# Gate loads moved to GpSimd's queue with five slots, three slots of gate scratch, and eight filler steps ahead of each attention loop, in a two-layer hybrid block

## The chip, the cores and the metric

The kernel runs on one core of one Trainium2 chip. The metric is the device time of one execution in microseconds; the number that stands for a kernel is the median of several runs. Engines are written as in the profile: PE (TensorE's matmuls), PEld (its weight loads), DVE (VectorE), ACT (ScalarE), POOL (GpSimd) and SP (SyncE, which only issues DMAs here).

## What is computed

Two layers of a hybrid block over 768 tokens (256 of context, 512 of latent), 1024 wide, in float32. Each layer projects the modulated input once, runs four mixers on slices of it, gates each by SiLU, and merges the four by per-channel sigmoid gates. In the second layer only the latent tokens are needed.

```python
def hybrid_layer(...):
    p = modulate(x, shift, scale) @ in_w          # split into the inputs of all four mixers
    oa = softmax_attention(mla_project(...))      # i=0, "mla"
    ob = rwkv_branch(...)                         # i=1, a scan over time in both directions
    oc = softmax_attention(gqa_project(...))      # i=2, "gqa"
    od = differential_attention(...)              # i=3, "diff": two softmaxes per head
    outs = [o * silu(gate) for o in (oa, ob, oc, od)]
    x_new = post_norm(ALPHA * x + gate_l * merge_branches(outs, logits, merge_b, branch_w, out_w))

def merge_branches(outs, gate_logits, merge_b, branch_w, out_w):
    g = jax.nn.sigmoid(gate_logits + merge_b)
    y = g[..., :D_MODEL] * (outs[0] @ branch_w[0])
    for i in range(1, N_BRANCH):
        y = y + g[..., i * D_MODEL:(i + 1) * D_MODEL] * (outs[i] @ branch_w[i])
    return y @ out_w
```

## The kernel before, in words

Every float32 product is made of three matmuls on a rounded high part and a low rest of each operand (`mm3`, L302; the same by hand in `m_block`, L539, and `m_stream`, L572). Weights come by DMA in pieces of 128x1024 on SP's queue; ACT rounds them (L292) and DVE takes the rest (L295).

A layer has three stages.

**Attention.** Three loops run one after the other, gqa, mla and diff. Ahead of each, `m_stream` projects its queries, keys and values (L572). In a loop PE transposes queries and keys (L601), makes scores (L647), DVE takes the row maximum (L650), ACT the exponential (L653), in the diff loop DVE combines two softmaxes (L962 to L964), PE transposes the weights (L669), ACT copies them (L671) and PE multiplies by the values (L694). Beside this runs a *filler*, one generator `fill()` for the whole stage: the input projections of the RWKV mixer (`t_block`, L302 with 256 or 512 columns, evicted at L986), in the first layer also the modulation for later (`ada`, L392), then the SiLU gates of the gqa and of the mla branch (`out_gate`, L539, 24 matmuls of 256 columns for each pair of token tiles and half of the weights). The filler has one PSUM bank, "F". `beside(loop, filler, FILL[l][n])` takes filler steps in proportion to the loop's steps; a step is 12 matmuls of 256 or of 512 columns, or 4 of L392. An order on each engine is then made by the scheduler from the order in which the program is traced: earlier traced goes first when both could.

**Scan.** The RWKV recurrence runs by an order of PE that is written out (`manual_schedule`), with a stream of other projections between its steps: the gates of diff (`out_gate` i=3) and of the scan's branch (`late_gate`), each with a scratch tile `oth`, and the merge gates (`merge_gates`), whose 32 tiles of 128x768 (128x512 in the second layer) are written to DRAM as `gd`.

**Merges.** `merge(i)` for i = 0, 2, 3, beside `rwkv_finish`, then i = 1. For each of eight column blocks j it loads the gate tile `th` from `gd` (three slots), every second j a weight tile `wb` (L1471; ACT L1472, DVE L1473), runs 12 matmuls of 384 columns (6 of 512 in the second layer) and lets DVE multiply by the gate (L1481 or L1483) and DVE or POOL add to `y` (L1484). At the end of `rwkv_finish` the tiles `h` are loaded on POOL's queue (L1654, six of 512 KB, four in the second layer), as soon as the memory of the scan is free. Then the output projection follows.

The change touches `out_gate`, `late_gate`, `merge` and `_run_layers`.

Of the kernel before, what the change touches and what calls it, by code (L numbers as in the profile page):

```python
# [10 lines left out]
F32 = mybir.dt.float32  # L11
F32R = mybir.dt.float32r
# [21 lines left out]
WBUFS = 5  # L34
LEAD = (6, 1, 6)
RATE = (2.15, 1.08)
# [176 lines left out]
class _Kernel:  # L213
# [1205 lines left out]
    def out_gate(self, l, i, O, toks, pool):  # L1419

        def use(t, g):
            th = self.t(pool, [128, 772 if pool is self.ep else 256], "E" if pool is self.ep else "oth")[:, :256]
            self.gate(th, g)
            self.nc.gpsimd.tensor_tensor(out=O[:, t], in0=O[:, t], in1=th, op=ALU.mult)
        yield from self.m_block(l, f"og{i}", toks, use)

    def late_gate(self, l, i, toks):

        def use(t, g):
            th = self.t(self.mp, [128, 256], "oth")  # L1430
            self.gate(th, g)
            self.nc.scalar.dma_start(out=self.gg[t], in_=th)
        yield from self.m_block(l, f"og{i}", toks, use)
# [14 lines left out]
    def merge(self, l, i, O, toks, y, first):  # L1448

        nc = self.nc  # L1450
        base, n = toks[0] * 128, len(toks) * 128
# [13 lines left out]
        for j in range(8):  # L1465
            th = self.t(self.mp, [128, n], "th", bufs=3)
            nc.sync.dma_start(out=th, in_=self.gd[i * 8 + j][:, :n])
            if j % 2 == 0:
                o = (i * 8 + j) * 256
                raw, wh, wl = (self.t(self.mp, [128, 512], f"wb{x}", F32R if x else F32, bufs=2) for x in range(3))  # L1470
                nc.sync.dma_start(out=raw, in_=self.a["brw"][l][:, o:o + 512])  # L1471
# [62 lines left out]
def _run_layers(K, only=None):  # L1534
# [18 lines left out]
    for l in range(DEPTH):  # L1553
# [23 lines left out]
        with mk(f"qk{l}", QB) as K.qp, mk(f"ep{l}", EB) as K.ep, mk(f"at{l}") as K.ap, \  # L1577
# [4 lines left out]
            filler = K.with_bank(fill(), "F")  # L1582

            def free():
                while K.wbusy:
                    next(filler, None)
            Qg = K.gq_proj(l, qt)
            Kg, Vg, kr = K.gkv_proj(l)
            O[2] = newO()
            beside(K.gqa_attn(qt, O[2], Qg, Kg, Vg), filler, FILL[l][0])  # L1590
            free()
            ready.add(2)
            m = K.mla_proj(l, qt, kr)
            O[0] = newO()
            beside(K.mla_attn(qt, O[0], *m), filler, FILL[l][1])
            free()
            ready.add(0)
            dd = K.diff_proj(l, qt)
            O[3] = newO()
            beside(K.diff_attn(l, qt, O[3], *dd), filler, FILL[l][2])  # L1600
            run(filler)
# [128 lines left out]
```

## Time and profile before

| | |
|---|---|
| median of 3 runs | 2085.11 us (2085.06 to 2086.12) |
| the profiled execution | 2084.66 us |
| its span on the core | 2082.9 us |
| PE busy | 1903.6 us (91%) |
| DVE busy | 1156.1 us (56%) |
| ACT busy | 816.6 us (39%) |
| POOL busy | 181.2 us (9%) |
| mean granted clock of TensorE | 0.962 |

The stages, in us from the span's start: first layer attention 50 to 531 (gqa loop from 84, mla from 245, diff from 383), scan to 980, merges to 1107, output projection to 1176; second layer attention 1200 to 1585 (gqa loop from 1239, mla from 1339, diff from 1482), scan to 1940, merges to 2026, output projection to the end. PE is busy almost everywhere, so the question at each place is how much of a stretch PE does not work, what it waits for, and at which clock it works.

### The profile page before, as it was taken

To read this page: it belongs to the slowest core of one execution; us is meant where nothing else is said; L and a number is where in the kernel's file an instruction comes from. 1 tells how busy PE (TensorE), PEld (TensorE's weight loads), DVE (VectorE), ACT (ScalarE), POOL (GpSimd) and SP (SyncE) were. 2 spreads that over 40 slices of the span, in tenths; PEclk is the share of its full clock that TensorE was granted. 3 is DMA by queue.
4 is the path that set the end of the run, shared out by engine and by line. 5 is a ranking of instruction groups with operands and counts; after the bars stand their busy time and mean duration, and the time that the engine had idled before them with its cause. 6 is when DMAs were issued, how large, how long until landed. Compare 5 with 4: busy or idle time off the path is not lost. (4 is left out here: it accounts for less than half of the span.)

```text
span 2082.9 us, 46213 instructions
## 1 busy us (share of the span) xinstructions
PE 1903.6 (91%) x19886; PEld 1575.2 (76%) x19886; DVE 1156.1 (56%) x2471; ACT 816.6 (39%) x1649; POOL 181.2 (9%) x303
## 2 busy tenths in 40 slices
PE   6899999888899999999788979999988999999877
PEld 4778878666788898888676677788877777777556
DVE  5554453576434433443878865454686444445677
ACT  3454462565323332332122236463665343233230
POOL 1000000000200000000130020000101000000120
PEclk9899999998899999999999889999998999999989
DMA  7110133310222222223743220111102222222651
GB/s 281 37 31 28 57 93 91 91 53 21 65 85 73 72 73 73 73 73 122 249 143 116 100 65 21 44 41 31 42 21 82 81 88 83 77 89 78 230 165 41
DMA packets 62614, 176.04 MB, mean 85 GB/s; under 512 B 7449, under 2 KB 12233, under 8 KB 62409
## 3 DMA queue, kind: packets, MB, share of 16 engines
q1 hardware_dynamic: 47144, 139.93, 21.4%
q10 hardware_dynamic: 13824, 27.90, 3.8%
q0 software_dynamic: 1440, 5.24, 0.6%
q8 instruction: 156, 2.56, 0.5%
q14 instruction: 50, 0.40, 0.1%
HBM read 145.50 MB, written 27.55 MB: 83 GB/s over the span
## 5 line engine op out<-in xcount | busy, mean ns | idle before, releaser
L302 PE MATMUL ps<-xh,wx 128*128 128x384 f32 (+2 forms) x3096 | 691.4, 368 | 4.0 <-ACT mth L1443 1.7
L302 PEld LDWEIGHTS ps<-xh,wx 128*128 128x128 f32 x3096 | 531.7, 189 | 65.8 <-issue 8.3
L292 ACT ACTIVATE wx<-wx 128x1024 fp32r<-128x1024 f32 (+2 forms) x94 | 98.3, 1046 | 307.1 <-PE ps L302 205.7
L295 DVE TENSOR_TENSOR wx<-wx,wx 128x1024 fp32r<-128x1024 f32 (+2 forms) x94 | 113.5, 1208 | 143.9 <-ACT wx L292 143.3
L650 DVE TENSOR_REDUCE nmax<-ps 128x1 f32<-128x768 f32 (+1 forms) x160 | 134.7, 846 | 54.8 <-PE ps L647 53.8
L572 PE MATMUL ps<-wx,xh 128*128 128x256 f32 (+1 forms) x1200 | 155.7, 288 | 7.6 <-DVE mu L1001 6.7
L302 PE MATMUL ps<-xh,wb 128*128 128x384 f32 (+1 forms) x576 | 134.3, 385 | 28.4 <-DVE th L1483 21.2
L572 PEld LDWEIGHTS ps<-wx,xh 128*128 128x128 f32 x1200 | 151.2, 191 | 9.6 <-ACT xc L476 6.8
L539 PE MATMUL ps<-wx,xh 128*128 128x256 f32 x960 | 139.9, 299 | 14.5 <-DVE oth L1417 7.4
L647 PE MATMUL ps<-qk,qk 128*128 128x384 f32 (+1 forms) x504 | 134.8, 371 | 16.7 <-ACT E L653 16.4
L653 ACT ACTIVATE E<-ps,nmax 128x768 f32<-128x768 f32 (+1 forms) x160 | 130.5, 817 | 44.2 <-DVE nmax L650 41.6
L302 PEld LDWEIGHTS ps<-xh,wb 128*128 128x128 f32 x576 | 107.6, 201 | 51.5 <-DVE th L1483 16.0
L539 PEld LDWEIGHTS ps<-wx,xh 128*128 128x128 f32 x960 | 128.7, 201 | 20.3 <-DVE oth L1417 7.8
L671 ACT ACTIVATE PH<-ps 128x512 f32<-128x512 f32 x156 | 91.1, 597 | 71.8 <-PE ps L669 71.3
L647 PEld LDWEIGHTS ps<-qk,qk 128*128 128x128 f32 x504 | 83.7, 195 | 40.7 <-ACT E L653 28.6
L1443 ACT ACTIVATE mth<-ps,hmb 128x384 f32<-128x384 f32 (+1 forms) x96 | 58.6, 611 | 113.1 <-PE ps L302 111.5
L669 PE MATMUL ps<-cstalways,E 128*128 128x128 f32 x624 | 99.9, 282 | 3.0 <-ACT PH L671 1.6
L694 PE MATMUL ps<-PH,V 128*64 128x256 f32 x624 | 88.1, 411 | 3.8 <-ACT PH L671 3.4
L669 PEld LDWEIGHTS ps<-cstalways,E 128*128 128x128 f32 x624 | 74.6, 144 | 15.9 <-ACT PH L671 4.6
L629 DVE TENSOR_TENSOR qk<-ps,qk 32x256 fp32r<-32x256 f32 (+5 forms) x104 | 59.3, 575 | 44.8 <-ACT qk L628 43.1
L295 DVE TENSOR_TENSOR wx<-wf,wx 128x1024 fp32r<-128x1024 f32 (+2 forms) x34 | 40.0, 1178 | 60.4 <-PE ps L302 33.8
L694 PEld LDWEIGHTS ps<-PH,V 128*64 128x64 f32 x624 | 41.8, 143 | 36.5 <-ACT PH L671 14.1
(325 smaller groups left out, 2782.2 us busy)
## 6 DMA issues: line engine op xcount, KB each, us to landing
wx<-in_inw_dram SPq DMA_DIRECT2D x88, 512.0 KB, 3.8
wf<-in_inw_dram SPq DMA_DIRECT2D x30, 512.0 KB, 3.6
wf<-in_adaw_dram SPq DMA_DIRECT2D x24, 512.0 KB, 3.6
gd<-mth ACTq DMA_DIRECT2D x32, 384.0 KB, 2.4
th<-gd SPq DMA_DIRECT2D x32, 384.0 KB, 3.2
adaw<-in_adaw_dram SPq DMA_DIRECT2D x16, 512.0 KB, 10.2
wx<-in_outw_dram SPq DMA_DIRECT2D x16, 512.0 KB, 4.8
wb<-in_brw_dram SPq DMA_DIRECT2D x32, 256.0 KB, 3.5
```

Of the source, the lines that this page charges most:

```text
L292: nc.scalar.activation(out=hi[:, :n], in_=raw[:, :n], func=AF.Copy)
L295: eng.tensor_tensor(out=lo[:, :n], in0=raw[:, :n], in1=hi[:, :n].bitcast(F32), op=ALU.subtract)
L302: self.nc.tensor.matmul(o, lhsT=w, rhs=x[:, s] if s is not None else x, start=first and p == 0, stop=last and p == 2)
L539: self.nc.tensor.matmul(ps[:, j * n:j * n + n], lhsT=self.xtok(x[k], s), rhs=w, start=k == 0 and p == 0 and j == 0, stop=k == 7 and p == 2 ...
L572: self.nc.tensor.matmul(ps, lhsT=self.xtok(x[k], s), rhs=w[:, c], start=k == 0 and p == 0 and head, stop=k == 7 and p == 2 and (tail or t ...
L629: nc.vector.tensor_tensor(out=lo[r, s], in0=ps[r], in1=hi[r, s].bitcast(F32), op=ALU.subtract)
L647: nc.tensor.matmul(o, lhsT=qt[:n, q], rhs=kt[:n, s], start=i == 0, stop=i == len(passes) - 1)
L650: nc.vector.tensor_reduce(out=nm, in_=v, axis=AX.X if ctx else AX.XY, op=ALU.max, negate=True)
L653: nc.scalar.activation(out=self.halves(e[:, :n], v), in_=v, func=AF.Exp, bias=nm, accum_out=den)
L669: nc.tensor.transpose(pt[:, c:c + 128], e[:, (k0 + k) * 128:(k0 + k) * 128 + 128], self.ident)
L671: nc.scalar.activation(out=hi, in_=pt, func=AF.Copy)
L694: nc.tensor.matmul(po[64 * (kk % 2):64 * (kk % 2) + 64, :n], lhsT=v2(kk), rhs=x[:, s], start=j == 0 and k < 2, stop=j == len(groups) - 1 a ...
```

## The change

Three things, in seven lines of code.

1. `LEAD` gets a fourth entry, 8, and a helper `ahead()` draws that many filler steps before each of the three attention loops, in both layers.
2. The scratch tile `oth` of the gates in the scan stage gets three slots instead of one.
3. In `merge`, the loads of the gate tiles `th` are issued on GpSimd's queue instead of SP's and get five slots instead of three; the high and low parts of the weight tile `wb` get three slots instead of two.

```diff
-LEAD = (6, 1, 6)
+LEAD = (6, 1, 6, 8)
...
     def out_gate(self, l, i, O, toks, pool):
...
-            th = self.t(pool, [128, 772 if pool is self.ep else 256], "E" if pool is self.ep else "oth")[:, :256]
+            th = self.t(pool, [128, 772], "E")[:, :256] if pool is self.ep else self.t(pool, [128, 256], "oth", bufs=3)
...
     def late_gate(self, l, i, toks):
...
-            th = self.t(self.mp, [128, 256], "oth")
+            th = self.t(self.mp, [128, 256], "oth", bufs=3)
...
     def merge(self, l, i, O, toks, y, first):
...
-            th = self.t(self.mp, [128, n], "th", bufs=3)
-            nc.sync.dma_start(out=th, in_=self.gd[i * 8 + j][:, :n])
+            th = self.t(self.mp, [128, n], "th", bufs=5)
+            nc.gpsimd.dma_start(out=th, in_=self.gd[i * 8 + j][:, :n])
...
-                raw, wh, wl = (self.t(self.mp, [128, 512], f"wb{x}", F32R if x else F32, bufs=2) for x in range(3))
+                raw, wh, wl = (self.t(self.mp, [128, 512], f"wb{x}", F32R if x else F32, bufs=3 if x else 2) for x in range(3))
...
+            def ahead():
+                for _ in range(LEAD[3]):
+                    next(filler, None)
...
+            ahead()
             beside(K.gqa_attn(qt, O[2], Qg, Kg, Vg), filler, FILL[l][0])
...
+            ahead()
             beside(K.mla_attn(qt, O[0], *m), filler, FILL[l][1])
...
+            ahead()
             beside(K.diff_attn(l, qt, O[3], *dd), filler, FILL[l][2])
```

Three places show how the order of the instructions changes.

PE at the start of the first layer's gqa loop, before. `ps_968` and `ps_1059` are filler (a projection of 256 and the next of 512 columns), `ps_913` and `ps_918` are query tiles and `ps_957` a key tile being transposed.

```order
L302 MATMUL ps_968<-xh_452,wx_964 128x256
L601 MATMUL ps_913<-cstalways_113,E_909 128x128 x2
L601 MATMUL ps_918<-cstalways_113,E_909 128x128 x4
L302 MATMUL ps_1059<-xh_239,wx_963 128x512
L302 MATMUL ps_1059<-xh_240,wx_963 128x512
L601 MATMUL ps_957<-cstalways_113,E_954 128x128 x2
```

The same place now; `ps_970` is the filler of 512 columns, `ps_993` and `ps_998` the queries, `ps_1014` the first keys.

```order
L302 MATMUL ps_970<-xh_387,wx_939 128x512
L302 MATMUL ps_970<-xh_386,wx_940 128x512
L601 MATMUL ps_993<-cstalways_113,E_989 128x128 x2
L601 MATMUL ps_998<-cstalways_113,E_989 128x128 x4
L302 MATMUL ps_970<-xh_437,wx_939 128x512
L302 MATMUL ps_970<-xh_438,wx_939 128x512
L302 MATMUL ps_970<-xh_437,wx_940 128x512
L302 MATMUL ps_970<-xh_452,wx_939 128x512
L302 MATMUL ps_970<-xh_453,wx_939 128x512
L302 MATMUL ps_970<-xh_452,wx_940 128x512
L601 MATMUL ps_1014<-cstalways_113,E_1011 128x128 x2
```

Of the 24 matmuls of 512 columns, 2 stood ahead of the first keys; now all 24 do, 18 of them ahead of the queries too. In the second layer the numbers are 0 ahead of the first keys and now 18, with the other 6 behind the first keys.

PE inside the second layer's diff loop, before. L539 is filler (a SiLU gate), the rest is the loop.

```order
L539 MATMUL ps_16394<-wx_16384,xh_13172 128x256
L647 MATMUL ps_16341<-qk_16112,qk_16152 128x384 x2
L539 MATMUL ps_16394<-wx_16383,xh_13174 128x256
L694 MATMUL ps_16283<-PH_16270,V_2663_15559 64x256 x2
L694 MATMUL ps_16283<-PH_16250,V_2663_15559 64x256 x2
L694 MATMUL ps_16283<-PH_16232,V_2663_15559 64x256 x2
L647 MATMUL ps_16365<-qk_16170,qk_16212 128x384
L601 MATMUL ps_16294<-cstalways_113,E_16290 128x128 x2
L601 MATMUL ps_16306<-cstalways_113,E_16290 128x128 x4
L647 MATMUL ps_16365<-qk_16170,qk_16212 128x384
L539 MATMUL ps_16394<-wx_16383,xh_13198 128x256
L539 MATMUL ps_16394<-wx_16384,xh_13198 128x256
```

The same heads and tiles now.

```order
L647 MATMUL ps_16593<-qk_16400,qk_16434 128x384 x2
L694 MATMUL ps_16545<-PH_16532,V_2680_15746 64x256 x2
L694 MATMUL ps_16545<-PH_16518,V_2680_15746 64x256 x2
L694 MATMUL ps_16545<-PH_16500,V_2680_15746 64x256 x2
L647 MATMUL ps_16617<-qk_16452,qk_16486 128x384
L601 MATMUL ps_16556<-cstalways_113,E_16552 128x128 x2
L601 MATMUL ps_16562<-cstalways_113,E_16552 128x128 x4
L647 MATMUL ps_16617<-qk_16452,qk_16486 128x384
```

The filler is gone from the whole of this loop: before, it held 24 matmuls of 256 columns (L302), 24 of 512 and 192 of L539; now the L302 stand in the gqa and mla stretches, 96 of the L539 at the end of the mla loop and the last 96 between the diff projection and its first keys. In the first layer's diff loop the filler (288 matmuls of L539, now with only 12 of L392 instead of 88) is drawn to the front: before, 60 of the loop's 80 score matmuls (L647) were issued when it ran out, now 23.

POOL at the end of `rwkv_finish` in the first layer, before; `th` does not appear as a load.

```order
L1142 TENSOR_TENSOR YT_5667<-YT_5667,bc_5529 128x512
L1654 DMA h_1850_11641<-in_xin_dram 128x1024
L1654 DMA h_1851_11643<-in_xin_dram 128x1024
L1654 DMA h_1852_11645<-in_xin_dram 128x1024
L1654 DMA h_1853_11647<-in_xin_dram 128x1024
L1654 DMA h_1854_11649<-in_xin_dram 128x1024
L1654 DMA h_1855_11651<-in_xin_dram 128x1024
L1484 TENSOR_TENSOR y_1779_11320<-y_1779_11320,th_11771 128x384 x2
```

The same place now; the loads `gd_22` and `gd_23` are those of the gates j = 4 and j = 5 of merge i=2.

```order
L1467 DMA th_11837<-gd_22_90 128x768
L1661 DMA h_1850_11641<-in_xin_dram 128x1024
L1661 DMA h_1851_11643<-in_xin_dram 128x1024
L1661 DMA h_1852_11645<-in_xin_dram 128x1024
L1661 DMA h_1853_11647<-in_xin_dram 128x1024
L1661 DMA h_1854_11649<-in_xin_dram 128x1024
L1661 DMA h_1855_11651<-in_xin_dram 128x1024
L1484 TENSOR_TENSOR y_1779_11320<-y_1779_11320,th_11771 128x384 x2
L1484 TENSOR_TENSOR y_1781_11322<-y_1781_11322,th_11817 128x384 x2
L1467 DMA th_11863<-gd_23_91 128x768
```

The gates j = 0 to 4 of merge i=2 are issued ahead of the `h` loads, the gate j = 5 behind them and behind two additions of `y`. In the second layer j = 0 to 5 stand ahead, j = 6 behind the loads and three additions.

## Rows read from the trace of the kernel before

**Rows 1.** Stretches: length, PE, PEld, DVE, ACT, POOL busy us, clock, DMA share, GB/s.

```profile
75.00:100.00 25.00, 16.20 (x91) 13.85 (x90) 15.50 (x41) 10.33 (x29) 1.71 (x6) 0.73 0.14 42
275.00:300.00 25.00, 24.97 (x177) 18.11 (x175) 14.79 (x30) 15.04 (x33) 0.00 (x0) 1.00 0.33 106
```

**Rows 2.** The same view of the two diff loops, and of a part of each.

```profile
385.00:499.00 114.00, 96.66 (x684) 76.12 (x684) 79.69 (x168) 71.09 (x156) 8.51 (x15) 0.93 0.22 66
499.00:524.00 25.00, 20.00 (x98) 12.45 (x98) 19.10 (x43) 16.76 (x38) 2.15 (x2) 0.73 0.14 42
1482.00:1585.00 103.00, 91.16 (x623) 73.83 (x622) 82.32 (x144) 73.56 (x153) 8.05 (x13) 0.95 0.09 26
...
1500.00:1525.00 25.00, 20.57 (x149) 16.73 (x147) 24.23 (x43) 20.09 (x42) 0.52 (x2) 0.99 0.08 22
```

**Rows 3.** Timeline of PE at both gqa starts: start, us, what, [idle before <-releaser].

```profile
83.89 1.46 PE L601 MATMUL ps<-cstalways,E 128*128 128x128 f32 x6 [2.38 <-ACT E L619]
...
92.62 0.69 PE L601 MATMUL ps<-cstalways,E 128*128 128x128 f32 x2 [6.42 <-DVE qk L629]
...
1242.54 0.65 PE L601 MATMUL ps<-cstalways,E 128*128 128x128 f32 x4 [0.65 <-ACT E L619]
1250.75 0.69 PE L601 MATMUL ps<-cstalways,E 128*128 128x128 f32 x2 [7.56 <-ACT E L619]
```

**Rows 4.** The same view: filler matmuls of 256 and 512 columns, at full clock.

```profile
1238.88 3.01 PE L302 MATMUL ps<-xc,wx 128*128 128x256 f32 x24
...
1284.14 1.67 PE L302 MATMUL ps<-xh,wx 128*128 128x512 f32 x6
1285.64 0.38 PE L703 MATMUL ps<-cstalways,E 128*128 128x128 f32 x2
...
1584.80 6.00 PE L539 MATMUL ps<-wx,xh 128*128 128x256 f32 x48
```

**Rows 5.** DVE by line and shape, 383 to 525: count, busy us, mean ns, idle before.

```profile
L650 DVE TENSOR_REDUCE nmax<-ps 128x1 f32<-128x768 f32 x32 | 30.1, 952 | 9.2 <-PE ps L647 9.0
...
L650 DVE TENSOR_REDUCE nmax<-ps 128x1 f32<-128x256 f32 x16 | 6.6, 416 | 3.2 <-PE ps L647 3.2
```

**Rows 6.** The same for PE, 383 to 525.

```profile
L392 PE MATMUL ps<-wf,cs 128*32 128x256 f32 x88 | 9.5, 435 | 1.5 <-DMA wf<-in_adaw_dram 1.5
```

**Rows 7.** The same for DVE, 1482 to 1585.

```profile
L650 DVE TENSOR_REDUCE nmax<-ps 128x1 f32<-128x768 f32 x32 | 30.4, 952 | 1.9 <-PE ps L647 1.6
...
L295 DVE TENSOR_TENSOR wx<-wf,wx 128x1024 fp32r<-128x1024 f32 x4 | 4.9, 1226 | 7.7 <-PE ps L572 7.5 <-issue 0.2
...
L1417 DVE SCALAR_TENSOR_TENSOR E<-E,ps 128x256 f32<-128x256 f32 x8 | 3.3, 414 | 1.1 <-ACT E L1416 1.0
...
L295 DVE TENSOR_TENSOR wx<-wx,wx 128x1024 fp32r<-128x1024 f32 x2 | 2.4, 1222 | 0.0
```

**Rows 8.** DVE's busy time in L650 alone, in one stretch of the first diff loop.

```profile
499.00:524.00 25.00, 9.20 (x13) 0.73 0.14 42
```

**Rows 9.** Timeline of PE in the gate stretch that opens the first scan.

```profile
546.68 9.64 PE L539 MATMUL ps<-wx,xh 128*128 128x256 f32 x60 [6.33 <-DVE oth L1417]
```

**Rows 10.** Waits of PE in both merge stages (975:1110, 1925:2030): us, times, longest.

```profile
PE ps L302 <- DVE th L1483: 11.0, 8, 3.4
...
PE ps L302 <- DVE th L1483: 10.2, 7, 4.1
```

**Rows 11.** Stretches around merge i=2 in both layers, columns as in rows 1.

```profile
1020.00:1052.00 32.00, 21.89 (x97) 19.85 (x97) 19.86 (x35) 2.80 (x5) 10.88 (x14) 0.84 0.69 243
...
1963.00:1985.00 22.00, 12.88 (x47) 8.64 (x47) 18.11 (x26) 6.96 (x10) 7.16 (x7) 0.93 0.89 320
```

**Rows 12.** POOL's and SP's issues beside it; GB/s in 40 slices of 1020:1052.

```profile
1023.16 3.34 POOL L1654 DMA_DIRECT2D h<-in_xin_dram  x6 [19.79 <-DVE O L1143]
1025.59 0.32 SPq L1467 DMA_DIRECT2D th<-gd  x1
...
GB/s 18 20 0 0 164 374 210 215 271 364 410 419 421 411 429 412 410 410 406 407 412 398 388 398 396 142 81 292 119 0 77 238 13 88 296 108 0 15 300 177
```

## The prediction

> **What bounds the kernel now.** I read stretches first, then single waits. In the middle of a gqa or mla loop PE is full: 24.97 of 25 us at full clock [rows 1]. A filler matmul there costs its whole time; it hides nothing and nothing hides it. The starts of the gqa loops are the opposite: PE works 16.20 of 25 us at a clock of 0.73 [rows 1], because the first transposes wait 2.38 and 6.42 us in the first layer and 0.65 and 7.56 us in the second [rows 3] for the keys to go through norm and rotation on DVE, POOL and ACT. The diff loops lie between: with filler PE is busy 96.66 of 114 us and 91.16 of 103 us; the first loop's last part, where its filler has run out, shows 20.00 of 25 us at 0.73, and the second loop has a stretch where DVE is busy 24.23 of 25 us [rows 2]. There the loop's own chain sets the pace, and filler sits partly in holes of PE. In the merges PE waits 11.0 and 10.2 us for the gate product [rows 10], with 10.1 of 32 us and 9.1 of 22 us idle around merge i=2 [rows 11].
>
> So the change is a trade. It moves filler to starts that are idle (gqa) and to starts that are not (mla, diff), and takes it from the end of the stage, the diff loops, where part of it was hidden.
>
> **The sum, part by part,** against the profiled execution, 2084.66 us; the median of the runs is 0.45 us above it.
>
> *gqa starts.* A 256-column filler matmul takes 0.125 us (3.01 for 24, or 6.00 for 48), a 512-column one 0.25 us (1.50 us from the start of six to what follows) [rows 4]. In each layer 18 of 512 now run ahead of the first transposes, 4.5 us, and 6 more close behind, 1.5 us; the gaps are 8.8 and 8.2 us [rows 3]. Against it, a weight split and the filler's own evictions now stand among DVE's and ACT's first steps of the loop, one or two us of delay; for it, PE should go cold for a shorter time. I take 4.5 us gained in each layer, 9 together (4 to 14). The mla starts have no gap worth filling: 0.
>
> *The second diff loop* loses all its filler: 24 matmuls of 256, 24 of 512 and 192 of 256 columns, 3 + 6 + 24 = 33 us of PE, which now stand in full stretches (what falls into the gqa gap is counted above). What is the loop worth without it? The trace does not show such a loop, so I bound it. DVE's own work is 82.3 us less the filler's weight splits and gates, 4.9 + 2.4 + 3.3, so 71.7 us [rows 2, 7]. At DVE's fullest, 24.23 of 25, that is 74 us; at the share of the filler-less stretch, 19.10 of 25, it is 94 us [rows 2]. The row maxima L650 give a third way: 30.4 us of them in the loop, 9.20 in the filler-less 25 us [rows 7, 8], so 83 us. I take 82, since it rests on a stretch without filler and both loops have the same kinds of steps. 33 + 82 - 103 = **+12 us** (+4 to +24).
>
> *The first diff loop* keeps 288 of its gates' matmuls (36 us) and gives up 76 of 88 L392, 9.5 x 76/88 = 8 us [rows 6], which now run in the full loops before it. The filler ends after 23 of 80 score matmuls, 7 of the 16 short row maxima and 8 of the 32 long ones: 10.5 of 36.7 us of L650 [rows 5]. The other 26.2 us of L650 at 9.20 per 25 us last 71 us [rows 8]; at DVE's fullest pace 56 us. I take 68, near the first, which is this loop. Ahead of that stand 37 us of filler, 29% of the loop's own PE work (116.7 - 45.5 = 71 us, so 21) and some 5 us of transposes that come early: 63 us, or 67 with a few holes left (74 at the density of 385 to 499). Before, the same ground took 139 us [rows 2]. 67 + 68 - 139 + 8 = **+4 us** (-12 to +14).
>
> *Gate scratch.* Three slots of `oth` let the second gate pass without the first's buffer, and the wait of 6.33 us [rows 9] ends early. The next group then needs its weights: their halves are made on ACT and DVE behind work that has not moved, so most of the time is waited for there. I take -1.5 us (-4 to 0); in the second layer the wait there is already for weights, 0.
>
> *Merges.* Each of the 32 gate tiles per layer now costs POOL an issue, 0.56 us by the six `h` loads (3.34 us) [rows 12], so 18 us a layer; POOL is 9% busy and its additions are needed only at the next merge, so this is hidden unless POOL stands still. POOL does stand still: a gate load waits there for its slot, and what is queued behind it are the additions of `y`, the `h` loads and, in both layers, the scaling of `rwkv_finish`. With five slots the slot comes free early enough for most. In the first layer gates j = 0 to 4 no longer come while the `h` loads fill the DMA engines at about 410 GB/s [rows 12]; j = 5 is issued behind 3 MB of `h`, 8 us at that rate, and behind two additions. The `h` loads start at 1023.16, so they end near 1033, about when j = 5 is wanted. Of 10.1 us idle [rows 11] I take 8 back (0 to 10). In the second layer j = 6 waits behind three additions, so some 3 us of wait come back, and DVE is busy 18.11 of 22 us [rows 11], which leaves little room: I take 4 (0 to 9). Together **-12 us**. The third slot of the `wb` halves ends only waits of ACT, whose cover is that PE runs behind it: 0.
>
> Sum: -9 + 12 + 4 - 1.5 - 12 = -6.5 us, so 2078.2 for a profiled execution and **2078.6 us** for the median.
>
> **Rivals.** *The diff loops starve* (slower). PE loses its clock when it works in short pieces: the filler-less stretch has 0.73 against 0.93 with filler [rows 2]. If both loops run at 19.10 us of DVE in 25, the second costs +24 and the first 67 + 71 - 139 + 8 = +7, and the sum is +8.5: 2093.6 us. It turns slower than before once the second loop without filler lasts over 88.5 us. For it: the only filler-less stretch of this trace. Against: that stretch is the end of a loop, where the chain drains.
>
> *The loops' own chain is quicker than that* (faster). At DVE's fullest pace the second loop costs +4 and the first 67 + 56 - 139 + 8 = -8: 2058.6 us at the end, some 2068 half way. For it: the stretch 1500 to 1525 reaches that pace with little filler in it. Against: ACT is 20.09 of 25 us busy there too, and each tile passes between both.
>
> *The merges gain nothing.* The gates and `h` now share one queue: j = 5 to 7 wait for all of `h` in one wait as long as the five before, and 12 us stay: 2090.6; with half of it, 2084.6. The Trainium skill, "DMA: Bandwidth & Descriptors", section "SWDGE vs HWDGE vs iDMA", says that GpSimd's DMAs and those of the other issuers feed different queues inside each DMA engine, which takes turns between them; by that, gates on SP's queue shared the engines with `h`, and gates on GpSimd's queue come after it. No row here shows a gate behind `h`, and by that rule the sum would be nearer 2084.6. Against the full price: five of eight gates are issued ahead of `h`.
>
> **How the numbers follow.** About 0.2%, 4 us, is what a measurement of this kernel tells from no change. Forecast 0.40 (2072 to 2085; 0.28 of it faster by over 0.2%, 0.12 within); starving diff loops 0.20 (slower); quicker loops 0.25 (faster); merges without gain 0.15 (0.11 within, 0.04 slower). So faster 0.53, within 0.23, slower 0.24. The range leaves out the far end of the quick loops and the last of the slow ones: 2063 to 2092.
>
> **What would show it.** gqa starts: 18 matmuls of 512 columns ahead of the first L601, and PE over 20 us in the first 25. The second diff loop: no L539 in it, 78 to 88 us from its first transpose to the last L703, PE about 17 us in 25. First diff loop: filler ends some 65 us after its start. Merges: PE's waits on L1483 near 3 us in the first layer and 5 in the second, one of them long, at j = 5 and j = 6. It is wrong if the loops without filler run at another pace than 9.20 us of L650 in 25, if the mla loops prove not to be full, or if POOL's queue holds back the scaling of `rwkv_finish` for long.

## The result and the profile after

The changed kernel takes 2130.89 us (median of 5 runs, 2129.97 to 2136.75) where the kernel before takes 2085.11 (5 runs beside it, 2080.18 to 2086.12): a ratio of 1.023, with a 95% interval of 1.0211 to 1.0249. It is slower by 46 us; 2078.6 us were forecast and 2092 was the upper end. The profiled execution took 2136.75 us, 52 us more than the profiled one before, and the working below goes by these two.

The page of the changed kernel, busy times and two of its DMA queues (packets, MB, share of 16 engines):

```profile
PE 1931.8 (90%) x19886; PEld 1598.6 (75%) x19886; DVE 1163.3 (54%) x2471; ACT 816.7 (38%) x1649; POOL 210.3 (10%) x367
...
q1 hardware_dynamic: 37928, 118.96, 17.7%
q0 software_dynamic: 6560, 26.22, 3.7%
```

PE's busy time has grown by 28 us, from 1903.6, although the same matmuls run. TensorE's mean granted clock fell from 0.962 to 0.951, and 1.2% of 1904 us would be an estimated 22 of these 28. Idle time of PE has grown by 24 us, from 179 to 203. Together these are the 52 us; where they arise is to be looked for stage by stage. The 26.22 MB on the software queue are the gates and `h`.

**Second layer's attention.** Stretches of the kernel before: gqa and mla together, diff projection, diff loop (columns as in rows 1: length, PE, PEld, DVE, ACT, POOL busy, clock, DMA share, GB/s).

```profile
1239.00:1424.10 185.10, 171.53 (x1048) 138.12 (x1046) 97.13 (x201) 101.31 (x205) 5.50 (x27) 0.96 0.12 34
1424.10:1482.70 58.60, 58.60 (x463) 55.38 (x463) 25.44 (x46) 19.06 (x36) 7.90 (x10) 1.00 0.18 53
1482.70:1584.80 102.10, 90.26 (x616) 72.93 (x615) 82.26 (x144) 72.86 (x151) 8.05 (x13) 0.95 0.09 27
```

The same of the changed kernel; the third row is the filler that now stands between projection and loop. The fourth is the loop, with only 12 filler matmuls behind its first transposes; the gate matmuls at its end belong to the next stage, as they do in the loop before.

```profile
1263.70:1486.80 223.10, 211.46 (x1268) 174.12 (x1267) 111.30 (x231) 112.06 (x221) 6.81 (x29) 0.94 0.12 34
1486.80:1532.90 46.10, 46.10 (x387) 46.10 (x386) 17.76 (x20) 11.60 (x22) 7.55 (x6) 1.00 0.20 58
1532.90:1545.10 12.20, 10.28 (x86) 10.07 (x85) 3.07 (x8) 3.93 (x10) 1.66 (x3) 1.00 0.17 50
1545.10:1632.90 87.80, 68.82 (x391) 47.10 (x389) 73.41 (x131) 66.20 (x139) 3.10 (x9) 0.86 0.04 13
```

Read the rows in pairs. gqa and mla grow by 38.0 us, and PE's busy time there by 39.9. Some 28 us of it are filler that came in (48 matmuls of 512 columns, 24 of 256 and 96 of L539, and 12 of L1039), paid in full; some 5 us are the mla loop's own last matmuls, which stood in the projection's row before; the rest is that the same matmuls take longer (L647 40.3 us instead of 37.8). The projection gives back 12.5 us: some 7 us of filler and these last matmuls. The diff loop, with its filler in front, gives back 2.1 us (102.1 to 12.2 + 87.8) for some 21 us of filler that left it: PE's busy time falls by only 11.2 (90.26 to 10.28 + 68.82), and PE's idle time grows from 11.8 to 20.9. At a granted clock of 0.86 where it was 0.95, the loop's own matmuls take longer (L647 24.2 us instead of 20.7, L601 15.8 instead of 13.0). That is the trade in one place: +38.0 - 12.5 - 2.1 = +23.4 us.

**First layer's attention.** gqa and mla grow from 242.2 to 255.6 us, of which 8 are the moved L392 (PE's busy time there grows by 8.3); diff projection and loop together stay at 205.4. Together +13.4. The first diff loop, filler half and filler-less half:

```profile
405.00:471.00 66.00, 60.10 (x449) 54.34 (x441) 42.18 (x89) 42.01 (x91) 9.03 (x15) 0.94 0.15 42
471.00:537.00 66.00, 51.29 (x251) 33.12 (x251) 56.29 (x121) 48.14 (x109) 1.25 (x3) 0.79 0.03 9
```

**The gqa starts.** Timeline of PE of the changed kernel (start, us, what, idle before and its releaser), which answers to [rows 3]:

```profile
84.27 6.02 PE L302 MATMUL ps<-xh,wx 128*128 128x512 f32 x18 [1.86 <-ACT E L986]
90.13 0.82 PE L601 MATMUL ps<-cstalways,E 128*128 128x128 f32 x6
...
93.48 0.44 PE L601 MATMUL ps<-cstalways,E 128*128 128x128 f32 x2 [1.13 <-DVE qk L629]
...
1267.05 4.48 PE L302 MATMUL ps<-xh,wx 128*128 128x512 f32 x18 [0.48 <-ACT E L986]
1271.37 0.60 PE L601 MATMUL ps<-cstalways,E 128*128 128x128 f32 x4
1275.61 0.44 PE L601 MATMUL ps<-cstalways,E 128*128 128x128 f32 x2 [3.64 <-ACT E L619]
...
1279.96 2.93 PE L647 MATMUL ps<-qk,qk 128*128 128x384 f32 x8 [0.56 <-DVE qk L629]
1286.35 2.72 PE L1039 MATMUL ps<-bones,E 128*128 128x2 f32 x12 [3.46 <-ACT E L1036]
```

The first layer's L1039 in the changed kernel, and below it the same in the kernel before:

```profile
100.67 2.72 PE L1039 MATMUL ps<-bones,E 128*128 128x2 f32 x12 [3.77 <-ACT E L1036]
...
114.70 1.43 PE L1039 MATMUL ps<-bones,E 128*128 128x2 f32 x12
```

The waits of 6.42 and 7.56 us for the keys are down to 1.13 and 3.64. But behind the first scores (L647) stands a new one, for ACT's L1036: 3.46 us here, and 3.77 us in the first layer. L1036 and L1039 belong to the filler (they make the norm of the RWKV keys, as soon as these are projected): they are in the step behind the eight drawn ahead. Before, L1039 came 14 us later in the first layer and its 12 matmuls took 1.43 us; now they take 2.72. PE works 18.50 of the loop's first 25 us in the first layer and 16.86 in the second; before, 17.82 and 16.27 (the first two rows are before, the last two now). The gap was filled and came back.

```profile
83.90:108.90 25.00, 17.82 (x86) 14.02 (x86) 16.30 (x38) 11.72 (x26) 1.52 (x2) 0.73 0.04 4
...
1239.00:1264.00 25.00, 16.27 (x93) 14.03 (x92) 15.95 (x36) 12.43 (x30) 1.63 (x5) 0.80 0.07 22
...
84.20:109.20 25.00, 18.50 (x76) 15.76 (x77) 16.22 (x47) 8.34 (x17) 1.70 (x5) 0.67 0.07 22
...
1263.70:1288.70 25.00, 16.86 (x82) 14.13 (x81) 16.44 (x35) 11.37 (x26) 1.54 (x4) 0.77 0.16 43
```

**Gate scratch.** PE's timeline in the gate stretch that opens the first scan. The wait of 6.33 us for `oth` [rows 9] is gone; the weights are waited for instead, and the whole stretch is 45.1 us where it was 41.8.

```profile
564.22 0.58 PE L539 MATMUL ps<-wx,xh 128*128 128x256 f32 x1 [4.27 <-ACT wx L292]
566.03 2.72 PE L539 MATMUL ps<-wx,xh 128*128 128x256 f32 x11 [1.23 <-DVE wx L295]
...
575.68 0.38 PE L539 MATMUL ps<-wx,xh 128*128 128x256 f32 x1 [3.38 <-ACT wx L292]
```

**Merges.** From their first matmul to the output projection's first: 124.4 us in the first layer (before 116.1) and 81.6 in the second (80.0). ACT's timeline at the start of the first layer's merges:

```profile
1012.30 0.63 ACT L1472 ACTIVATE wb<-wb 128x512 fp32r<-128x512 f32 x1 [8.41 <-DMA wb<-in_brw_dram]
1012.84 0.58 ACT L1460 ACTIVATE xh<-ps 128x512 fp32r<-128x512 f32 x1
```

PE waits for that L1460, and SP's rows show when the weight tile was asked for (the third issue of L1471, at 1001.96):

```profile
1013.47 0.69 PE L302 MATMUL ps<-xh,wb 128*128 128x384 f32 x1 [7.05 <-ACT xh L1460]
...
998.48 2.57 SPq L1669 DMA_DIRECT2D gt<-gg  x5
1001.96 0.61 SPq L1471 DMA_DIRECT2D wb<-in_brw_dram  x1
```

Here five loads `gt` (L1669, the gate of the scan's branch, wanted later) are issued ahead of this tile, beside the five gate loads on GpSimd's queue, and ACT can start on it only 10 us after its issue. In the second layer PE waits longest for the gate j = 6, which is loaded behind `h` and three additions on POOL, and at the start for L277, a step of `rwkv_finish` that stands on DVE behind another late weight tile (DVE waits 4.24 us for ACT's L1472, which waits 5.99 us for its load):

```profile
2004.12 10.03 PE L302 MATMUL ps<-xh,wb 128*128 128x512 f32 x36 [4.44 <-DVE grs L277]
...
2041.15 1.97 PE L601 MATMUL ps<-cstalways,O 128*128 128x128 f32 x8 [6.53 <-DVE th L1483]
```

PE's waits over the whole span (us, times, longest). The first line is the kernel before, where the other three were 1.5, 0.8 and 1.3 us; the rest is the changed kernel.

```profile
PE ps L302 <- DVE th L1483: 21.2, 15, 4.1
...
PE ps L302 <- DVE th L1483: 12.9, 10, 3.0
PE ps L601 <- DVE th L1483: 8.2, 4, 6.5
PE ps L302 <- ACT xh L1460: 7.2, 2, 7.0
PE ps L302 <- DVE grs L277: 4.4, 1, 4.4
```

So the wait that the extra slots were for did shrink, by 8 us, and 16 us of other waits came.

The sum over the stages, in us: attention +13.4 and +23.4, gate stretches +3.3 and +0.6, scans -2.5 and +1.8, merges +8.3 and +1.6, the rest +2: 52.

### The profile page after: what moved, and what is told of

It reads as the page before. It is cut to its first block, busy times and chain, and to the rows that moved or that the text cites. A ratio compares the mean times of both kernels' runs of the same rounds, so it can differ in the third digit from the quotient of the medians.

```text
span 2135.0 us, 46183 instructions
## 1 busy us (share of the span) xinstructions
PE 1931.8 (90%) x19886; PEld 1598.6 (75%) x19886; DVE 1163.3 (54%) x2471; ACT 816.7 (38%) x1649; POOL 210.3 (10%) x367
## 3 DMA queue, kind: packets, MB, share of 16 engines
q0 software_dynamic: 6560, 26.22, 3.7%
## 5 line engine op out<-in xcount | busy, mean ns | idle before, releaser
L302 PE MATMUL ps<-xh,wx 128*128 128x384 f32 (+2 forms) x3096 | 687.8, 369 | 3.8 <-ACT E L986 2.5
L302 PEld LDWEIGHTS ps<-xh,wx 128*128 128x128 f32 x3096 | 535.8, 190 | 65.5 <-ACT E L986 4.5
L650 DVE TENSOR_REDUCE nmax<-ps 128x1 f32<-128x768 f32 (+1 forms) x160 | 135.2, 847 | 61.9 <-PE ps L647 61.0
L302 PE MATMUL ps<-xh,wb 128*128 128x384 f32 (+1 forms) x576 | 133.1, 387 | 31.5 <-DVE th L1483 12.9
L647 PE MATMUL ps<-qk,qk 128*128 128x384 f32 (+1 forms) x504 | 142.6, 390 | 18.1 <-ACT E L653 15.6
L572 PEld LDWEIGHTS ps<-wx,xh 128*128 128x128 f32 x1200 | 151.6, 192 | 9.4 <-ACT xc L476 6.7
L539 PE MATMUL ps<-wx,xh 128*128 128x256 f32 x960 | 139.3, 300 | 18.0 <-ACT wx L292 11.5
L302 PEld LDWEIGHTS ps<-xh,wb 128*128 128x128 f32 x576 | 110.5, 206 | 51.1 <-DVE th L1483 12.3
L539 PEld LDWEIGHTS ps<-wx,xh 128*128 128x128 f32 x960 | 127.6, 201 | 24.6 <-ACT wx L292 12.1
L647 PEld LDWEIGHTS ps<-qk,qk 128*128 128x128 f32 x504 | 89.3, 207 | 45.8 <-ACT E L653 27.5
```

The costliest lines, as they stand in the source:

```text
L302: self.nc.tensor.matmul(o, lhsT=w, rhs=x[:, s] if s is not None else x, start=first and p == 0, stop=last and p == 2)
L539: self.nc.tensor.matmul(ps[:, j * n:j * n + n], lhsT=self.xtok(x[k], s), rhs=w, start=k == 0 and p == 0 and j == 0, stop=k == 7 and p == 2 ...
L572: self.nc.tensor.matmul(ps, lhsT=self.xtok(x[k], s), rhs=w[:, c], start=k == 0 and p == 0 and head, stop=k == 7 and p == 2 and (tail or t ...
L647: nc.tensor.matmul(o, lhsT=qt[:n, q], rhs=kt[:n, s], start=i == 0, stop=i == len(passes) - 1)
L650: nc.vector.tensor_reduce(out=nm, in_=v, axis=AX.X if ctx else AX.XY, op=ALU.max, negate=True)
```

## The experiments

All are compared with the kernel before on the same chip; a ratio stands with its 95% interval, and the difference in us is between the medians. Some kernels have one line less ahead of the line in question, so that L1038 is L1039, L646 is L647 and so on.

### Which part costs: the three parts alone

Eight steps ahead of each loop, nothing else:

```diff
+            def ahead(n):
+                for _ in range(n):
+                    next(filler, None)
...
+            ahead(8)
             beside(K.gqa_attn(qt, O[2], Qg, Kg, Vg), filler, FILL[l][0])
...
+            ahead(8)
             beside(K.mla_attn(qt, O[0], *m), filler, FILL[l][1])
...
+            ahead(8)
             beside(K.diff_attn(l, qt, O[3], *dd), filler, FILL[l][2])
```

> Part 1 alone: eight filler steps ahead of each attention loop, nothing else changed. Theory A (the parts add up as the two traces show them by stage): the attention stages grow by about 13 us in the first layer and 24 us in the second, the merges stay as they were before (116 us from their first to the output projection's first matmul in the first layer, 80 in the second): about 2122 us, plus 37. Rival B (the parts disturb each other, so that the merges are slower because the stages ahead of them end at other times): the merges change here too, and the sum is near that of the whole change, 2131.

Measured: 2114.82 us against 2082.29, 1.0161 (1.0141 to 1.018), +33 us. In its profiled execution attention takes 9.5 us longer in the first layer and 23.8 in the second, and the merges do not grow (115.6 and 76.8 us).

Merges alone:

```diff
-            th = self.t(self.mp, [128, n], "th", bufs=3)
-            nc.sync.dma_start(out=th, in_=self.gd[i * 8 + j][:, :n])
+            th = self.t(self.mp, [128, n], "th", bufs=5)
+            nc.gpsimd.dma_start(out=th, in_=self.gd[i * 8 + j][:, :n])
...
-                raw, wh, wl = (... bufs=2) for x in range(3))
+                raw, wh, wl = (... bufs=3 if x else 2) for x in range(3))
```

> Part 3 alone: the gate tiles on GpSimd's queue in five slots, and three slots for the split weight. Theory A: the merges alone lose what they lose in the whole change, 8 us in the first layer and 2 in the second, with a wait of about 7 us of PE on the transposed operand at the first merge; 2095 us. Rival B, the forecast's own: alone they gain 12 us, 2073 us, and only the shifted stages ahead of them spoilt it.

Measured: 2096.22 us, 1.0064 (1.0044 to 1.0083), +14 us. ACT's timeline at the start of its first layer's merges shows the same row as the changed kernel, a weight tile taken up ahead of L1460, for whose load ACT waits:

```profile
996.47 0.63 ACT L1472 ACTIVATE wb<-wb 128x512 fp32r<-128x512 f32 x1 [7.03 <-DMA wb<-in_brw_dram]
997.00 0.58 ACT L1460 ACTIVATE xh<-ps 128x512 fp32r<-128x512 f32 x1
```

Three slots of gate scratch alone (`bufs=3` in `out_gate` and `late_gate`):

> Part 2 alone: three slots of gate scratch. Theory A: the wait of 6.33 us before the first layer's third gate group goes, but two waits for weights of about 4 us each take its place, so plus 0 to plus 4 us, 2085 to 2089. Rival B, the forecast's own: minus 1.5 us, 2083.6.

Measured: 2082.45 us, 0.9998 (0.9982 to 1.0014): nothing. The three ratios add to 1.022, and the whole is 1.023, so the parts can be studied one by one.

### Which start costs

One `ahead(8)` alone, ahead of gqa, of mla or of diff:

> Eight filler steps ahead of the gqa loop alone, in both layers. Theory A (what stands ahead of the loop also pulls the filler's own evictions and its norm of k, L1036 and L1039, into the loop's start, where PE waits for them): the gaps of 8.8 and 8.2 us at the two starts are filled but about 4 us of new wait stand at L1039 in each layer, and eight steps fewer are left for the diff loops: plus 5 to plus 15 us, 2090 to 2100. Rival B, the forecast's own: minus 9 us at the starts and plus 4 in the diff loops, about 2080.

Measured: 2090.55 us against 2082.29, 1.0062 (1.0042 to 1.0083), +8 us by the medians and 13 by the ratio. PE waits for L1036 behind the first scores, 3.63 us at 101.18 and 4.23 us at 1260.27, as in the changed kernel. In its profiled execution the first layer's attention takes 2 us less than before and the second layer's 9 us more. How much of that is the ninth step is taken apart below.

> Eight filler steps ahead of the mla loop alone. Theory A (the three places add up: 34 less 13 for gqa and 12 for diff): plus 6 to plus 12, of which most is cover missing in the diff loops. Rival B (they do not add up): within 3 us.

Measured: 2097.33 us against 2083.51, 1.0064 (1.004 to 1.0088), +14. In its profiled execution, in the second layer, gqa and mla take 12.6 us longer, and diff projection and loop give back 5.

> Eight filler steps ahead of the diff loop alone, in both layers: the same steps that the loop held before are drawn to its start, nothing moves between the loops. Theory A (a filler matmul inside a diff loop is mostly hidden by the loop's own chain on DVE and ACT, and costs its full time ahead of it): 8 steps of 12 matmuls are 11.7 us of PE that stand bare, the loops give back only part of it: plus 4 to plus 8 us in the second layer, 0 to plus 4 in the first; 2086 to 2094. Rival C (the place of filler in the diff loops does not matter, the loss comes from the starts alone): 2082 within 3 us.

Measured: 2093.96 us against 2081.89, 1.0055 (1.0036 to 1.0073), +12. From the end of the diff projection to the loop's last transposes it is 154.3 us instead of 148.4 in the first layer and 107.5 instead of 102.4 in the second. In the first layer some of it is the filler's own waiting: the steps drawn ahead there are L392, whose weight load (3.00 us) and sums (0.78 and 0.69) PE waits for ahead of the loop's first transposes. The three add to 1.8%, where all three together gave 1.6%. The filler is finite: whichever loop gets more, the diff loops get less.

### Filling the gap without moving filler to later or earlier loops

The eight steps stay ahead of gqa, and the loop owes them: its account begins at -8, so that the same number of steps as before has been drawn when it ends.

```diff
-def beside(first, second, rate):
-    due = 0.0
+def beside(first, second, rate, due=0.0):
...
+            ahead(8)
-            beside(K.gqa_attn(qt, O[2], Qg, Kg, Vg), filler, FILL[l][0])
+            beside(K.gqa_attn(qt, O[2], Qg, Kg, Vg), filler, FILL[l][0], due=-8.0)
```

> Eight filler steps ahead of the gqa loop, but the loop owes them: it draws none until its rate has paid for eight. So the gap at the start is filled, the ninth step (the filler's own evictions with L1036 and L1039) comes when it came before, and as many steps are left for the diff loops as before. Theory A (the loss of the run with eight steps ahead of gqa came from the early ninth step and from the steps missing later): minus 3 to minus 10 us against before. Rival C (a filled start is not worth anything, since the loop's first scores wait for the keys either way and what is moved to the gap was free where it stood): within 3 us of before.

Measured: 2075.98 us against 2081.89, 0.9954 (0.9933 to 0.9975): **faster by 0.46%**, some 10 us by the ratio and 6 by the medians. Its timeline of PE, at both gqa starts:

```profile
83.27 4.49 PE L301 MATMUL ps<-xh,wx 128*128 128x512 f32 x18 [1.73 <-ACT E L985]
...
93.19 0.44 PE L600 MATMUL ps<-cstalways,E 128*128 128x128 f32 x2 [4.08 <-DVE qk L628]
...
1246.78 0.44 PE L600 MATMUL ps<-cstalways,E 128*128 128x128 f32 x2 [3.46 <-ACT E L618]
```

The keys are waited for 4.08 and 3.46 us instead of 6.42 and 7.56, and no L1038 stands behind the first scores. The granted clock of the first 25 us is 0.93 in both layers (83.30:108.30 and 1235.10:1260.10), where it was 0.73 and 0.80. In the profiled execution the first layer's scan starts 4 us earlier and the second layer adds 3 to 4.

Now the same eight steps, owed one loop later, in mla: gqa has them on top of its own, so that the ninth step comes early, but the diff loops keep their filler.

```diff
+            ahead(8)
             beside(K.gqa_attn(qt, O[2], Qg, Kg, Vg), filler, FILL[l][0])
...
-            beside(K.mla_attn(qt, O[0], *m), filler, FILL[l][1])
+            beside(K.mla_attn(qt, O[0], *m), filler, FILL[l][1], due=-8.0)
```

> Eight filler steps ahead of the gqa loop, owed in the mla loop and not in the gqa loop: the ninth step, with the filler's evictions and L1036 and L1039, stands at the start of the gqa loop as in the change, but the diff loops keep all their filler. Theory A1 (the loss of eight steps ahead of gqa, plus 13, against minus 10 when owed at once, comes mostly from the steps missing in the diff loops): minus 2 to minus 8 us against before. Theory A2 (it comes mostly from the early ninth step): plus 3 to plus 12.

Measured: 2084.8 us against 2084.41, 1.0007 (0.9989 to 1.0026): neither gain nor loss. Its timeline of PE has the wait for ACT again:

```profile
99.20 2.72 PE L1038 MATMUL ps<-bones,E 128*128 128x2 f32 x12 [3.63 <-ACT E L1035]
...
1257.36 2.67 PE L1038 MATMUL ps<-bones,E 128*128 128x2 f32 x12 [4.17 <-ACT E L1035]
```

By the ratios the three stand at -0.5%, 0.1% and 0.6%. So of the 1.1% (22 us) between owed at once and never owed, about half goes with the ninth step that comes early and about half with the filler that is missing later. The first half also holds what it costs the mla loop to begin without filler, which no run shows by itself. The waits themselves, 3.63 + 4.17 = 7.8 us, and the slower L1038, 1.2 us each, would make most of the first half.

Is there a gain in more filler for the second diff loop? The second layer's rates lowered from (0.5, 0.4, 0.5) to (0.42, 0.33, 0.8), nothing else:

> The opposite of the change in the second layer: the filler's rates are set from 0.5, 0.4, 0.5 to 0.42, 0.33, 0.8 in the gqa, mla and diff loop, so that more filler is left for the diff loop and less is spent in loops where PE is full. Theory A (a filler matmul costs its full time in the gqa and mla loops and is mostly hidden in the diff loop): minus 3 to minus 10 us. Rival C (the diff loop's holes are filled already): within 3 us, or plus.

Measured: 2084.01 us, 1.0003 (0.9985 to 1.0022). No: its diff loop takes 120 us instead of 102, and the stages ahead of it 15 us less. The 33 us that it had fill its holes, and more gives nothing.

### Slots, queue and weight tiles apart

Five slots of `th`, still on SP's queue, two weight slots:

```diff
-            th = self.t(self.mp, [128, n], "th", bufs=3)
+            th = self.t(self.mp, [128, n], "th", bufs=5)
```

> Of part 3 only the slots: the gate tiles stay on SP's queue, in five slots instead of three; the split weight stays at two. Theory A (five gate tiles asked for at once stand ahead of the first weight tile of the merge in the same DMA engines, and the queue of the issuer matters less): the first merge of the first layer waits longer than before, later merges less: minus 4 to plus 4 us. Rival D (the queue is what hurts: behind POOL's additions and beside the h loads): the slots alone gain 5 to 12 us, as the forecast had it for both.

Measured: 2071.98 us against 2081.89, 0.9951 (0.9931 to 0.997): **faster by 0.49%**, 10 us. The first layer's merges take 107.6 us instead of 116, the second's 75.4 instead of 80, and PE's wait for the gate product over the span falls from 21.2 us to 12.2:

```profile
PE ps L302 <- DVE th L1483: 12.2, 9, 3.6
```

The other half, GpSimd's queue with three slots:

```diff
-            nc.sync.dma_start(out=th, in_=self.gd[i * 8 + j][:, :n])
+            nc.gpsimd.dma_start(out=th, in_=self.gd[i * 8 + j][:, :n])
```

> Of part 3 only the queue: the gate tiles on GpSimd's queue, still in three slots; the split weight stays at two. Theory A: with fewer tiles asked for at once the first weight tile comes sooner, but each gate tile is now issued behind POOL's additions of y two columns later, so PE waits for DVE's gate product more often: plus 10 to plus 30 us. Rival D (the queue is what hurts in part 3, whatever the slots): about the plus 13 us of part 3 alone. Rival E (the queue does no harm, the loss of part 3 is that of five slots): within 4 us of before.

Measured: 2092.7 us against 2081.89, 1.0047 (1.0031 to 1.0063), +11 us. POOL's timeline in the first layer shows how:

```profile
1024.72 2.61 POOL L1654 DMA_DIRECT2D h<-in_xin_dram  x5
1027.34 2.00 POOL L1484 TENSOR_TENSOR y<-y,th 128x384 f32<-128x384 f32 x2
1029.25 0.57 POOL L1467 DMA_DIRECT2D th<-gd  x1
1032.31 1.06 POOL L1467 DMA_DIRECT2D th<-gd  x2 [2.49 <-DVE y L1484]
1040.17 1.95 POOL L1484 TENSOR_TENSOR y<-y,th 128x384 f32<-128x384 f32 x2 [6.80 <-DVE th L1483]
```

The gates that merge i=2 wants are issued behind `h` and behind additions; then POOL stands still for 6.80 us, since the addition that is next waits for a gate product. PE waits 7.41 us at 1040.23 and, in the second layer, 7.55 us at 1994.84, both for DVE's L1483; over the span this wait grows to 26.1 us.

GpSimd's queue with five slots, but two weight slots:

> Part 3 without the third slot of the split weight: gate tiles on GpSimd's queue in five slots. Theory D (the queue costs, whatever the rest): GpSimd's queue at three slots cost 10 us, SP's at five slots gained 10; here plus 8 to plus 15, with the wait at the sixth or seventh gate of the second merge. Theory F (the third slot of the split weight puts a wait for a weight tile ahead of the first merge's operand on ACT, 4 to 7 us, and is the larger part): minus 5 to plus 5.

Measured: 2087.05 us against 2084.41, 1.0016 (0.9995 to 1.0037), +3 us, on the edge of what can be told. The wait for L1460 is 0.2 us; that for L277 stays, 4.8 us (1.3 with five slots on SP's queue), so it goes with the queue. So of the 14 us of the merges' part some 10 hang on the third weight slot. Is that slot bad by itself? SP's queue, five slots, three weight slots:

> Five slots for the gate tiles on SP's queue, and three slots for the split weight. Theory G (the third weight slot hurts by itself: it lets ACT take up a later weight tile ahead of the last transposed operand of a merge, and wait there for its load): the gain of 10 us of the slots alone is lost, within 4 us of before. Theory H (it hurts only beside GpSimd's queue): minus 8 to minus 12.

Measured: 2070.9 us against 2083.51, 0.994 (0.9922 to 0.9957), -13 us: no. ACT takes the weight tile ahead of L1460 here as well, but waits only 1.28 us for it:

```profile
990.10 0.63 ACT L1472 ACTIVATE wb<-wb 128x512 fp32r<-128x512 f32 x1 [1.28 <-DMA wb<-in_brw_dram]
990.64 0.58 ACT L1460 ACTIVATE xh<-ps 128x512 fp32r<-128x512 f32 x1
```

Here the third tile is issued at 987.46, ahead of all `gt` loads (as in the kernel before and with five slots alone), and ACT starts on it 2.6 us later. The third slot costs where the five gate loads go out from another queue and SP's queue has five `gt` loads ahead of that tile, and nothing where gates and weights leave one queue in the order in which they are wanted.

### The two good halves together

Owed steps ahead of gqa and five slots on SP's queue:

> The two edits that were faster alone, together: eight owed filler steps ahead of the gqa loop, and five slots for the gate tiles on SP's queue. If they work at different places (the gqa starts, the merges) they add up: minus 16 to minus 21 us, 2061 to 2066. If the one is paid back by the other, about minus 10.

Measured: 2061.5 us (median of 6) against 2084.41, 0.9896 (0.9864 to 0.9928): **22 us faster than the kernel before**, and the two gains add up.

The same with owed steps ahead of mla and diff too:

> Eight filler steps ahead of all three loops, each loop owing its eight before it draws more, and five slots on SP's queue. If owing takes the whole loss away at mla and diff too, the time is that of eight owed steps ahead of gqa alone with the same slots, 2061.5 us or a little less. If steps drawn to the start of the diff loop cost what they cost without owing (12 us, since nothing there moves between loops), it is 2070 to 2076.

Measured: 2080.93 us against 2083.51, 0.9986 (0.9972 to 1.0001). Owed steps at the other two starts cost 18 us against the kernel above. In the profiled executions 15 us of it lie in the first layer's attention: its diff loop's first transposes stand 11 us later (390.69 instead of 379.59), and from there to the last ones it takes 151.6 us instead of 147.3. A part of the 11 us is the filler's own waiting, as in the run with eight steps ahead of diff:

```profile
385.39 0.97 PE L391 MATMUL ps<-wf,cs 128*32 128x256 f32 x8 [3.24 <-DMA wf<-in_adaw_dram]
```

With the two waits behind it (0.76 and 0.69) that is 4.7 us ahead of transposes that could have run at once, since the kernel above starts them right behind the projection. Why the rest does not come back is not settled.

## Why the prediction was wrong, point by point

Term by term, forecast against the profiled execution: attention of the first layer -0.5 (gqa start -4.5, diff loop +4) against +13.4; of the second +7.5 (-4.5 + 12) against +23.4; gate stretches -1.5 against +3.9; merges -12 against +9.9; the scans and the rest 0 against +1.3. The steps that failed are the price of GpSimd's queue for the gates and of the third weight slot beside it, both put at nothing, which turned the merges' gain into a loss (22 of the 58 us), and the price of the steps drawn ahead, which left out the step behind them and undersized the loops that lose their filler (30 of the 58).

**What bounds the kernel: right.** Middle of gqa and mla full, gqa starts idle, diff loops paced by their chain. "A filler matmul there costs its whole time" is what the second layer's rows show: +39.9 us of PE, +38.0 us of time, 28 us of it filler.

**gqa starts, -9: the gap and its worth were right, the change was not what was costed.** Owed to the same loop, eight steps gain some 10 us. The prediction looked at the eight steps drawn ahead and not at the one behind them: `beside` goes on drawing at its rate, so the ninth stands at the loop's start and brings L1036 on ACT and L1039 on PE, for which PE waits 3.77 and 3.46 us. The granted clock of these 25 us is 0.67 and 0.77; owed it is 0.93. "PE over 20 us in the first 25" came out as 18.50 and 16.86.

**Second diff loop, +12: undersized, in the length of the loop without filler.** 82 us were taken from L650's pace in one filler-less stretch, and the loop takes 87.8. With the 12.2 us in front it is 100.0 where the prediction's terms make 94. DVE works 73.41 us of it, 20.9 in 25, between the two paces that served as bounds. That is 6 us; the other 10 us that the second layer's attention is above its forecast (+23.4 against -4.5 + 12 = +7.5) lie in gqa and mla: the gap that didn't close, 4.5, and filler, ninth step and scores (L647 40.3 us instead of 37.8) at a colder clock, 0.94 instead of 0.96.

**First diff loop, +4: right within its bounds.** Its filler ends at 469, 69 us after the projection and 61 us after the loop's first transposes, where some 65 was said, and the part behind it takes 69 us up to the next stage's first gate matmul, where 68 was said. Projection and loop together stay as they were (-4 was said), and the 8 us of L392 are in the loops before: +8. At the loop's start PE waits 3.27 us (404.58) for the weight load of the L392 drawn ahead, which had no price. The 13.4 us of the first layer are these 8, and a gqa start that lost instead of gaining.

**mla starts, 0: wrong.** The filler alone that this start draws costs 0.64%, 14 us: the stretches that it is drawn into pay for it in full, and the diff stretch that it left gives back 5 of 12.6 us in the second layer. The prediction counted what the diff loops lose once, for all three starts, in the two loops; but together these three starts cost 33 us, not 7.

**Gate scratch, -1.5: within its bounds (-4 to 0) alone, 0.** The reason given, that weights are waited for next, is what the rows show. Inside the whole change the stretch is even 3 us longer, with the weights later by as much.

**Merges, -12: the slots were right, the queue wrong.** Five slots on SP's queue gain 10 us. The prediction's price for GpSimd's queue was nothing "unless POOL stands still". It said that POOL does, and named what is queued there: `h`, the additions, and j = 5 and j = 6 behind them. These are the gates that came late (6.53 us at j = 6 in the second layer, where 3 us of wait were to come back), but POOL's standing still was given no price. The Trainium skill, "DMA: Bandwidth & Descriptors", section "SWDGE vs HWDGE vs iDMA", was cited for GpSimd's DMAs and the other issuers' having queues of their own, which take turns. The runs agree with the direction that the prediction drew from it, gates on SP's queue better beside `h` (at five slots 0.9951 on SP's queue against 1.0016 on GpSimd's, each to the kernel before), but they can't tell that mechanism from the order on POOL, which the rows show directly.

**The third weight slot, 0: wrong beside GpSimd's queue, right beside SP's.** It was to end "only waits of ACT, whose cover is that PE runs behind it": the cover was gone, since a weight tile that may be taken up earlier stands on ACT ahead of L1460, which PE needs (7.05 us).

**Rivals.** "The diff loops starve" was to decide from 88.5 us for the second loop; it took 87.8, so by its own condition it did not decide, and its end of 2093.6 is 37 us short. "Merges gain nothing" came nearest in kind; it had no loss in it. What the range lacked was a case in which a part turns its sign through something that it pulls in: the ninth step, the weight tile ahead of L1460.

**What stays open.** Why that weight tile's load lands up to 8.4 us after ACT could have taken it: five gate loads and five `gt` loads are issued ahead of it, which the rows show, but which of them delays it was not measured by itself. What the mla loop loses by beginning without filler, and why owed steps ahead of diff do not come back beyond the filler's own waits, no run shows.

## What to carry to other kernels

Fill a start that is idle with work, but make the loop behind it owe that work (at the starts of mla and diff even owed steps cost 18 us); otherwise a finite filler is taken from a later loop whose holes it was filling for nothing, and 21 us of filler removed from such a loop shorten it by 2. When work is drawn ahead, look at the first step behind it, since that one moves too. Give a load more slots before giving it another queue, and don't put it on an engine whose queue holds the consumers of that same data.

## What the runs showed of the hardware

- Loops that lose their filler lost clock with it here: a granted clock of 0.86 over 87.8 us in which PE is busy 68.82, against 0.95 over 102.1 us with 90.26 busy, and 0.79 over the 66 us with 51.29 busy in the first layer. The loop's own matmuls took longer at it (L647 24.2 us instead of 20.7), and PE's busy time fell by 11 us where 21 us of matmuls had left.
- The starts of the gqa loops (25 us) were granted a clock of 0.73 and 0.80 before, 0.67 and 0.77 with eight steps ahead, 0.93 in both layers with eight owed steps. The 12 matmuls of L1039 took 2.72 us in the second of these, and 1.43 us at 114.70 in the kernel before.
- An issue of a gate load occupies POOL for 0.57 us (at 1029.25 with GpSimd's queue and three slots), and SP for 0.32 [rows 12].
- How late a load lands here: the third 256 KB weight tile of the first merges could be used 10 us after its issue with five gate loads on another queue and five `gt` loads ahead of it, and 2.6 us after it with gates and weights on one queue.
